# A pool of its own for the second merge's matrices, and two buffers in other PSUM banks for the transposed v, in a hybrid gated-DeltaNet and retention block

## The chip, the cores and the metric

One core of a Trainium2 chip. The metric is the device time of one execution in microseconds (us). Times come from repeated executions and from one profiled execution, whose trace gives every instruction's start, length and cause of waiting. TensorE is PE in what follows (PEld its weight loads), VectorE DVE, ScalarE ACT, GpSimd POOL; SP issues most DMAs.

## The reference, cut to what matters

The layer normalises and projects 1280 tokens (256 of context, 1024 latent), runs a gated delta rule over one group of four heads and a retention over another, projects back, and ends in a SwiGLU. The change sits in the delta rule, between its projections and its scan:

```python
def gated_delta_rule(q, k, v, g, beta):
    ...
    kb = kc * bc[..., None]
    A = jnp.where(strict, jnp.einsum('nbhid,nbhjd->nbhij', kb, kc) * decay, 0.0)
    rhs = jnp.concatenate([vc * bc[..., None], kb * jnp.exp(G)[..., None]], axis=-1)
    sol = lax.linalg.triangular_solve(A + jnp.eye(CHUNK, dtype=A.dtype), rhs,
                                      left_side=True, lower=True, unit_diagonal=True)
    u, w = sol[..., :dv], sol[..., dv:]
    qk = jnp.einsum('nbhid,nbhjd->nbhij', qc, kc) * decay
    ...
    S0 = jnp.zeros((b, h, dk, dv), q.dtype)
    _, o = lax.scan(step, S0, (u, w, q_dec, qk, k_dec, g_last))
```

## The kernel before

The kernel cuts the sequence into ten chunks of 128 tokens and builds, for each chunk, head and direction, a unit triangular 128x128 matrix whose inverse the scan needs. A scheduler in the kernel's language decides the order of the instructions on each engine from the program's text, its pools and its own costs; each engine then runs its list in that order and waits on semaphores. All buffers are tiles of pools; a tag with `bufs=1` has one place, which the next user of the tag gets when every reader of the last one is done.

The stretch that matters lies between the projections of k, q and the retention gate (until about 274 us) and the scan:

- `pre(t)`, once for each chunk. PE multiplies k by itself into PSUM tile `kk` (L665), transposes q into `qt` (L670) and multiplies q by k into `kq` (L675). SP loads a row of decays `gw`; POOL makes the exponent `e` of it (L683, L685), ACT its exponential (L687). DVE multiplies `kk` by `e` into `ut` (L695, four instructions of 128x128 for each direction) and `kq` by `e` into `sp` (L697). `ut` goes to `un` in DRAM, `sp` to the scan's data `sd`. The loads and `gw`, `e`, `sp` live in pool GP.
- `invert(b)`, once for each of three batches of chunks, BATCH = [[0,1,2,9],[3,8,4,7],[5,6]]. Blocks of 32x32 of `un` are reloaded as `yr`, 128 blocks at a time one to a partition, and 31 steps of two DVE instructions (L730, L732) each invert all of them into X. X and its transpose XT go to DRAM `xd` in four stores (L736).
- `merge(b)`, once for each batch. It loads the batch's matrices into tile `U` (L747, up to 2 MB), clears `t64`, and puts the inverted blocks over both with four loads each (L751 into `U`, L752 into `t64`). Then PE joins blocks of 32 to 64 (L771, a DVE copy `xt` L774, L778 and L781) and of 64 to 128 (L794, `xt` L795, L798), ACT copies the results back into `U`, and `U` goes to `sd`. `U` and `t64` have `bufs=1` in pool GM for all three merges.
- Meanwhile the V phase: for each head PE convolves v (L576 to L578, eight weight tiles in three products), DVE adds four taps (L586), ACT applies the silu, PE transposes the result into `vT` (L820), ACT scales it into `vt` (L823) and stores it. `vT` lies in the PSUM banks of `kk`, `qt`, `kq` and the merges (`bank_b`); `vt` has one buffer.
- What can fill PE while it waits: the token-major projections of the output gate and of the retention (L842, L944, L946), matmuls `tm` of 128x256 (L341 to L343), which stand later in the program's text but depend on nothing here but their weights `whi`, `wlo`. 1,276 of them are left at 274 us and are done before the scan is half through. Their three banks are `bank_a`. ACT or DVE reads each out into `res`.

The scan's first loads of `sd` (tile `pk`) follow the merges.

Of the kernel before, what the change touches and what calls it, by code (L numbers as in the profile page):

```python
# [8 lines left out]
F32 = mybir.dt.float32  # L9
# [8 lines left out]
P = 128  # L18
# [7 lines left out]
H = 4  # L26
# [11 lines left out]
def build(nc, tc, ap, dbg=None, stop=None, marks=None):  # L38
# [3 lines left out]
    def pool(name, bufs=1, side=None, space=None):  # L42
        kw = {}
        if side is not None:
            kw["side"] = side
        if space is not None:
            kw["space"] = space
        if space is not DRAM:
            kw["reuse_waits"] = "tile"
        es = ExitStack()  # L50
        p = es.enter_context(tc.tile_pool(name=name, bufs=bufs, **kw))
        root.push(es)
        p_close[id(p)] = es
        return p
# [3 lines left out]
    def close(p):  # L58
        p_close.pop(id(p)).close()
# [5 lines left out]
    def checkpoint(name):  # L65
        if dbg is not None:
            marks.append((name, int(nc.cur_bb.bb.instructions[-1].name.split("-")[-1])))
        if stop == name:
            raise Stop()
# [16 lines left out]
    def bank(tag, name):  # L86
        return PS["pool"].tile([P, 512], F32, tag=tag, name=name, bufs=PS["tags"][tag])

    def bank_a(name):
        return bank("pa", name)  # L90

    def bank_b(name):
        return bank("pb", name)
# [67 lines left out]
    try:  # L161
# [363 lines left out]
        def c8(t, d):  # L525
            return slice(t * 8 + d * 4, t * 8 + d * 4 + 4)
# [17 lines left out]
        ps = bank_b("G")  # L544
# [14 lines left out]
        ps = bank_b("GT")  # L559
# [5 lines left out]
        CV = pool("cv", side="right")  # L565
# [61 lines left out]
        def load(pl, src, tag, bufs, shape=(P, H, P)):  # L627
            x = pl.tile(list(shape), F32, tag=tag, name=tag, bufs=bufs)
            SY.dma_start(x, src)
            return x  # L630
# [17 lines left out]
        checkpoint("rg")  # L648
        close(R2)
        close(W2)  # L650
        GP = pool("gp")
        GU = pool("gu")
        GI = pool("gi")

        BATCH = [[0,1,2,9],[3,8,4,7],[5,6]]
        where = {t: (b, c) for b, ch in enumerate(BATCH) for c, t in enumerate(ch)}
# [3 lines left out]
        def pre(t):  # L660
            b, c = where[t]
            kc = load(GP, kd[t], "kc", 2)
            pk = bank_b("kk")
            for h in range(H):
                T.matmul(pk[:, h * P:(h + 1) * P], kc[:, h, :], kc[:, h, :], start=True, stop=True)  # L665
            if t >= 2:
                qc = load(GP, qd[t - 2], "qc", 2)
                pn = bank_b("qt")
                for h in range(H):
                    T.transpose(pn[:, h * P:(h + 1) * P], qc[:, h, :], ident)  # L670
                for h in range(H):
                    S.activation(pn[:, h * P:(h + 1) * P], pn[:, h * P:(h + 1) * P], AF.Square, accum_out=nq[:, t - 2, h:h + 1])
                pq = bank_b("kq")
                for h in range(H):
                    T.matmul(pq[:, h * P:(h + 1) * P], kc[:, h, :], qc[:, h, :], start=True, stop=True)  # L675
            for d in range(2):
                gw = GP.tile([P, H, P], F32, tag="gw", name="gw", bufs=2)
                SY.dma_start(gw.rearrange("p h i -> p (h i)"),
                             grow_d[c8(t, d), :].rearrange("a b -> (a b)").partition_broadcast(P))
                e = GP.tile([P, H, P], F32, tag="e", name="e", bufs=2)  # L680
                for h in range(H):
                    col = t * 8 + d * 4 + h
                    G.tensor_scalar(e[:, h, :], gw[:, h, :], sm["nG"][:, col:col + 1], 1.0, ALU.add, ALU.mult)  # L683
                sg = 1 if d == 0 else -1
                G.affine_select(out=e, in_=e, compare_op=ALU.is_ge, fill=NEG, base=0,  # L685
                                pattern=[[0, H], [sg, P]], channel_multiplier=-sg)
                S.activation(e, e, AF.Exp)  # L687
                if t >= 2:
                    sp = GP.tile([P, 2, H, P], F32, tag="sp", name="sp", bufs=2)
                ut = GU.tile([P, H, P], F32, tag="ut", name="ut", bufs=2)  # L690
                for h in range(H):
                    col = t * 8 + d * 4 + h
                    hs = slice(h * P, (h + 1) * P)
                    abc_ = sm["ab"][:, col:col + 1]
                    V.scalar_tensor_tensor(ut[:, h, :], pk[:, hs], abc_, e[:, h, :], ALU.mult, ALU.mult)  # L695
                    if t >= 2:
                        V.scalar_tensor_tensor(sp[:, 0, h, :], pq[:, hs], abc_, e[:, h, :], ALU.mult, ALU.mult)  # L697
                SY.dma_start(un[b][:, 1 - d, c * H:(c + 1) * H, :], ut)
                if t >= 2:
                    S.activation(gw, gw, AF.Exp)  # L700
                    G.tensor_tensor(sp[:, 1], gw, qc, ALU.mult)
                    SY.dma_start(sd[t, :, 8 - 8 * d:10 - 8 * d], sp.rearrange("p a h i -> p a (h i)"))
# [5 lines left out]
        def invert(b):  # L708
# [4 lines left out]
            xd = xds[b] = dr.tile([4 * nb, 1024], F32, tag="xd%d" % b, name="xd%d" % b)  # L713
            yr = GI.tile([P, 1024], F32, tag="yr", name="yr", bufs=1)
            for k in range(4):
                SY.dma_start(yr[k:2 * nb:4].rearrange("r (i j) -> r i j", j=32),
                             un[b][q32[k]].rearrange("i e u j -> (e u) i j")[:, :, q32[k]])
            L = GI.tile([P, 1024], F32, tag="L", name="L", bufs=3)
            X = GI.tile([P, 1024], F32, tag="X", name="X", bufs=2)
            G.memset(X, 0.0)  # L720
# [4 lines left out]
            for j in range(31):  # L725
                n = 31 - j
                tmp = GI.tile([P, 256], F32, tag="tmp%d" % b, name="tmp", bufs=2)
                t3 = tmp[:2 * nb, :n * (j + 1)].rearrange("p (i c) -> p i c", c=j + 1)
# [3 lines left out]
                V.tensor_tensor(xs, xs, t3, ALU.subtract)  # L732
            XT = GI.tile([P, 1024], F32, tag="L", name="XT", bufs=3)
            V.tensor_copy(m(XT), X[:2 * nb].rearrange("p (i j) -> p j i", j=32))
# [3 lines left out]
        def blocks(b):  # L738

            nu = len(BATCH[b]) * H  # L740
            nb = 4 * nu

            def blk(dram, k):
                return dram.rearrange("(u b) (i j) -> b i u j", b=4, j=32)[k]

            uu = GM.tile([P, 2, len(BATCH[b]), H, P], F32, tag="U", name="U%d" % b, bufs=1)
            SY.dma_start(uu.rearrange("p e c h j -> p e (c h) j"), un[b])  # L747
            tt = GM.tile([P, 2, nu, 64], F32, tag="t64", name="t64", bufs=1)
            G.memset(tt, 0.0)
            for k in range(4):  # L750
                SY.dma_start(uu[q32[k]].rearrange("p e c h j -> p (e c h) j")[:, :, q32[k]], blk(xds[b][:2 * nb], k))  # L751
                SY.dma_start(tt[q32[k]].rearrange("p e u j -> p (e u) j")[:, :, (k % 2) * 32:(k % 2) * 32 + 32],  # L752
                             blk(xds[b][2 * nb:], k))
            return uu, [uu[:, 1 - d] for d in range(2)], [tt[:, d] for d in range(2)]

        def merge(b):
# [11 lines left out]
            for n in range(nu):  # L768
                for d, p, a, bb in pairs:
                    ca = (a % 2) * 32  # L770
                    T.matmul(ps1[q[bb], n * 32:n * 32 + 32], u[d][q[a], n, q[bb]], t[d][q[a], n, ca:ca + 32],  # L771
                             start=True, stop=True)
            xt1 = GM.tile([P, 16, 32], F32, tag="xt1", name="xt1", bufs=1)
            V.tensor_scalar(xt1.rearrange("p n j -> p (n j)")[:, :nu * 32], ps1[:, :nu * 32], -1.0, None, ALU.mult)  # L774
# [14 lines left out]
            for n0 in range(0, nu, 8):  # L789
                ps1, ps2 = bank_b("m2"), bank_b("m2")  # L790
                xt2 = GM.tile([P, 8, 64], F32, tag="xt2", name="xt2", bufs=1)
                for n in range(8):
# [21 lines left out]
        for h in range(H):  # L814
            y = newy()
            conv_block(8 + h, y, False)
            for t0, n in ((0, 2), (2, 4), (6, 4)):
                ps = bank_b("vT")
                for t in range(t0, t0 + n):
                    T.transpose(ps[:, (t - t0) * P:(t - t0 + 1) * P], y[:, t * P:(t + 1) * P], ident)  # L820
                vt = CV.tile([P, 4, P], F32, tag="vt", name="vt", bufs=1)
                for t in range(n):
                    S.activation(vt[:, t], ps[:, t * P:(t + 1) * P], AF.Copy, scale=sv3[:, t0 + t, h:h + 1])  # L823
                S.dma_start(vd[t0:t0 + n, :, h, :].rearrange("t p j -> p t j"), vt[:, :n])
# [1 line left out]
        checkpoint("v")  # L826
        RP = pool("rp", side="right")
        rope = RP.tile([P, TT, P], F32, tag="rope", name="rope")
        GM = pool("gm")
        for t in BATCH[2]:  # L830
            pre(t)
        checkpoint("pre2")
        merge(0)
        SY.dma_start(rope, ap["rope"])
# [7 lines left out]
            token_major(g, LAT, fin_gate, S, W)  # L842
        checkpoint("rgz")
        close(GM)
        close(GI)
        close(GU)
        close(GP)


        SC = pool("sc", bufs=2, side="right")  # L850
# [764 lines left out]
```

## Time and profile before

| | us |
|---|---|
| three executions | 1484.93, 1485.49, 1488.77 (median 1485.49) |
| the profiled execution | 1486.29 |
| its span, first to last instruction | 1484.5 |
| PE busy | 1406.9 (95% of the span) |
| DVE busy | 974.2 (66%) |
| POOL busy | 628.4 (42%) |
| ACT busy | 604.9 (41%) |
| mean granted TensorE clock | 0.977 of full |

The profiled execution's 1486.29 us is 1.8 us more than its span, and 0.80 us above the median of the three. A span is read by its engines' shares first, and then stretch by stretch: an engine at 95% over the whole has its idle time in a few places, and those are the places where a new order can matter.

### The profile page before, as it was taken

The page shows a single profiled execution, that of the slowest core. Times are in us where ns is not written, and L with a number is a line of the kernel's source. Part 1 is how long each engine was busy: PE and PEld are TensorE (multiplying, and loading weights), DVE is VectorE, ACT ScalarE, POOL GpSimd, SP SyncE. Part 2 cuts the span into 40 slices and gives each one's busy share as a digit, 9 for nine tenths or more (in the row PEclk, how much of TensorE's full clock was granted, in tenths as well). Part 3 has the DMA queues.
Part 4 walks back from the last instruction along what each step waited for, and adds up shares of the span by engine and source line. Part 5 has one row for each costly group of instructions (what it writes and reads, how often), then busy time and mean ns, then how long its engine had stood idle before and what let it go on. Part 6 is the DMA issues. An engine that isn't in the chain of part 4 may idle for free.

```text
span 1484.5 us, 24226 instructions
## 1 busy us (share of the span) xinstructions
PE 1406.9 (95%) x8919; PEld 1206.4 (81%) x8919; DVE 974.2 (66%) x1938; ACT 604.9 (41%) x1268; POOL 628.4 (42%) x581
## 2 busy tenths in 40 slices
PE   7999999987988899999799899999999999999997
PEld 2798888976878899999688688777888888788886
DVE  6566788269868345689767876656555555657486
ACT  5543564375541121245534533323333333444454
POOL 0120011377124343234134689899555553335321
PEclk9999999998999899999899999999999999999999
DMA  8536686578597755996633265765222242776863
GB/s 321 208 99 212 188 250 202 165 233 273 175 266 204 248 186 205 414 361 221 204 114 114 85 207 215 258 243 183 106 107 107 106 144 79 237 278 190 308 204 114
DMA packets 176567, 298.16 MB, mean 201 GB/s; under 512 B 43496, under 2 KB 93880, under 8 KB 172096
## 3 DMA queue, kind: packets, MB, share of 16 engines
q1 hardware_dynamic: 124896, 253.17, 49.5%
q10 hardware_dynamic: 49072, 35.83, 7.7%
q0 software_dynamic: 2480, 7.60, 1.4%
q8 instruction: 70, 1.15, 0.3%
q14 instruction: 49, 0.40, 0.1%
HBM read 206.60 MB, written 89.96 MB: 200 GB/s over the span
## 4 chain that ended last, share of the span: by engine, by line
PE 42%; POOL 4%; DMA 2%; DVE 1%; issue 1%; ACT 0%; SPq 0%; POOLq 0%; ACTq 0%; DVEq 0%
PE ffn L1306 7%; PE ffn L1305 7%; PE ffn L1304 7%; PE fo L1432 4%; PE fo L1430 4%; PE fo L1431 4%; PE op L1163 2%; PE op L1164 2%; PE op L1165 2%; DMA wd<-tw 1%; POOL ws L1277 1%; POOL tw L1358 1%; POOL tw L1357 1%; DVE wlo L315 1%; POOL tw L1359 0%
## 5 line engine op out<-in xcount | busy, mean ns | idle before, releaser
L341 PE MATMUL tm<-whi,hhi 128*128 128x256 f32 (+1 forms) x704 | 201.1, 289 | 5.6 <-ACT xa L354 1.6
L342 PE MATMUL tm<-wlo,hhi 128*128 128x256 f32 (+1 forms) x704 | 201.3, 288 | 0.6 <-DVE wlo L315 0.6
L343 PE MATMUL tm<-whi,hlo 128*128 128x256 f32 (+1 forms) x704 | 199.2, 287 | 0.0
L341 PEld LDWEIGHTS tm<-whi,hhi 128*128 128x128 f32 x704 | 134.0, 191 | 10.0 <-ACT xa L354 2.4
L1304 PE MATMUL ffn<-t,whi 128*128 128x512 f32 x352 | 137.0, 390 | 2.0 <-ACT whi L314 2.0
L1306 PE MATMUL ffn<-t,wlo 128*128 128x512 f32 x352 | 137.1, 390 | 1.5 <-DVE wlo L315 1.5
L1305 PE MATMUL ffn<-t,whi 128*128 128x512 f32 x352 | 137.0, 389 | 0.0
L314 ACT ACTIVATE whi<-wraw 128x512 fp32r<-128x512 f32 (+2 forms) x98 | 75.2, 771 | 151.4 <-PE ffn L1305 80.5
L342 PEld LDWEIGHTS tm<-wlo,hhi 128*128 128x128 f32 x704 | 134.6, 191 | 1.8 <-DVE wlo L315 1.1
L343 PEld LDWEIGHTS tm<-whi,hlo 128*128 128x128 f32 x704 | 134.1, 192 | 1.8 <-issue 0.9
L314 ACT ACTIVATE whi<-ws 128x512 fp32r<-128x512 f32 x88 | 55.6, 632 | 175.4 <-PE ffn L1305 121.6
L315 DVE TENSOR_TENSOR wlo<-ws,whi 128x512 fp32r<-128x512 f32 x88 | 94.3, 1073 | 47.7 <-ACT whi L314 47.5
L1430 PE MATMUL fo<-whi,ahi 128*128 128x512 f32 x308 | 119.3, 390 | 1.3 <-ACT ahi L314 1.3
L1431 PE MATMUL fo<-wlo,ahi 128*128 128x512 f32 x308 | 119.9, 389 | 0.0
L1432 PE MATMUL fo<-whi,alo 128*128 128x512 f32 x308 | 119.0, 390 | 0.0
L315 DVE TENSOR_TENSOR wlo<-wraw,whi 128x512 fp32r<-128x512 f32 (+2 forms) x92 | 100.3, 1092 | 25.0 <-ACT whi L314 25.0
L1304 PE MATMUL ffn<-b,whi 128*128 128x512 f32 x264 | 103.9, 393 | 4.1 <-ACT whi L314 4.1
L1306 PE MATMUL ffn<-b,wlo 128*128 128x512 f32 x264 | 103.9, 394 | 1.1 <-DVE wlo L315 1.1
L1305 PE MATMUL ffn<-b,whi 128*128 128x512 f32 x264 | 103.8, 393 | 0.0
L576 PE MATMUL b<-hhi,whi 128*128 128x512 f32 (+1 forms) x256 | 96.3, 376 | 1.5 <-ACT y L580 1.5
L578 PE MATMUL b<-hhi,wlo 128*128 128x512 f32 (+1 forms) x256 | 95.2, 372 | 0.0
L577 PE MATMUL b<-hlo,whi 128*128 128x512 f32 (+1 forms) x256 | 94.9, 371 | 0.0
(427 smaller groups left out, 3494.6 us busy)
## 6 DMA issues: line engine op xcount, KB each, us to landing
adaw<-ada_w SPq DMA_DIRECT2D x48, 512.0 KB, 4.6
pk<-sd SPq DMA_DIRECT2D x16, 1536.0 KB, 10.1
wraw<-wfi SPq DMA_DIRECT2D x44, 512.0 KB, 4.0
ar<-ad SPq DMA_DIRECT2D x33, 512.0 KB, 4.7
w<-wfo SPq DMA_DIRECT2D x22, 512.0 KB, 4.6
wd<-tw SPq DMA_DIRECT2D x11, 1024.0 KB, 4.8
ad<-act SPq DMA_DIRECT2D x20, 512.0 KB, 3.0
raw<-wd SPq DMA_DIRECT2D x20, 512.0 KB, 4.9
```

The source lines that it names most:

```text
L314: S.activation(hi, raw, AF.Copy)
L315: e.tensor_tensor(lo, raw, hi.bitcast(F32), ALU.subtract)
L341: T.matmul(o, hhi[:, k, tsl], whi[:, k % 4, :], start=(k == 0), stop=False)
L342: T.matmul(o, hhi[:, k, tsl], wlo[:, k % 4, :], start=False, stop=False)
L343: T.matmul(o, hlo[:, k, tsl], whi[:, k % 4, :], start=False, stop=(k == KT - 1))
L576: T.matmul(o, whi[:, k, :], hh, start=(k == 0), stop=False)
L1304: T.matmul(o, whi[:, k, :], xhi(xn, slice(0, 4), k), start=(first and k == 0), stop=False, **kw)
L1305: T.matmul(o, whi[:, k, :], xlo(xn, slice(0, 4), k), start=False, stop=False, **kw)
L1306: T.matmul(o, wlo[:, k, :], xhi(xn, slice(0, 4), k), start=False, stop=(k == 3), **kw)
L1430: T.matmul(po[g][i], ahi[:, ts], whi, start=(j == 0 and not kw), stop=False, **kw)
L1431: T.matmul(po[g][i], ahi[:, ts], wlo, start=False, stop=False, **kw)
L1432: T.matmul(po[g][i], alo[:, ts], whi, start=False, stop=(j == FH - 1), **kw)
```

## The change

It does four things, all in the stretch described. The pools on the left side are opened in the order GU, GI, GP, so that GP is the last; after the last `pre` GP is closed and a new pool G2 opened in its place. The second merge takes its `U` and `t64` from G2 and no longer shares the one place in GM. GM moves to the right side. The transposes `vT` go to `bank_a`, the three banks of the projections, and `vt` has two buffers.

```diff
-        GP = pool("gp")
         GU = pool("gu")
         GI = pool("gi")
+        GP = pool("gp")
...
-            uu = GM.tile([P, 2, len(BATCH[b]), H, P], F32, tag="U", name="U%d" % b, bufs=1)
+            at = G2 if b == 1 else GM
+            uu = at.tile([P, 2, len(BATCH[b]), H, P], F32, tag="U", name="U%d" % b, bufs=1)
             SY.dma_start(uu.rearrange("p e c h j -> p e (c h) j"), un[b])
-            tt = GM.tile([P, 2, nu, 64], F32, tag="t64", name="t64", bufs=1)
+            tt = at.tile([P, 2, nu, 64], F32, tag="t64", name="t64", bufs=1)
...
-                ps = bank_b("vT")
+                ps = bank_a("vT")
...
-                vt = CV.tile([P, 4, P], F32, tag="vt", name="vt", bufs=1)
+                vt = CV.tile([P, 4, P], F32, tag="vt", name="vt", bufs=2)
...
-        GM = pool("gm")
+        GM = pool("gm", side="right")
         for t in BATCH[2]:
             pre(t)
+        close(GP)
+        G2 = pool("g2")
...
         close(GM)
+        close(G2)
         close(GI)
         close(GU)
-        close(GP)
```

Every engine has the same instructions as before; only their order changes. It is the same up to the end of the retention gate's projections and again from the output projection of the delta rule on. Line numbers below the first new line are higher by one, and below the new pool by three.

On PE, at the end of the V phase (`b` is the convolution's bank, `vT` the transposed v), before:

```order
L577 MATMUL b_4048<-hlo,whi 128x512
L578 MATMUL b_4048<-hhi,wlo 128x512
L820 MATMUL vT<-ident,y 128x128 x4
L341 MATMUL tm<-whi,hhi 128x256 x3
L342 MATMUL tm<-wlo,hhi 128x256
L343 MATMUL tm<-whi,hlo 128x256
```

and now:

```order
L821 MATMUL vT<-ident,y 128x128 x10
L665 MATMUL kk<-kc 128x128 x4
L670 MATMUL qt<-ident,qc 128x128 x4
L675 MATMUL kq<-qc,kc 128x128 x4
L665 MATMUL kk<-kc 128x128 x4
L670 MATMUL qt<-ident,qc 128x128 x4
L675 MATMUL kq<-qc,kc 128x128 x4
L821 MATMUL vT<-ident,y 128x128 x10
L341 MATMUL tm<-whi,hhi 128x256
L342 MATMUL tm<-wlo,hhi 128x256
L343 MATMUL tm<-whi,hlo 128x256
```

Before, the first projections `tm` stand among the convolutions, 22 of the 40 transposes and the last two chunks' `kk`, `qt`, `kq` come later among `tm`. Now all of the V phase and all ten chunks stand ahead of the first `tm`; behind these rows 232 `tm` follow in a block, and then merge 0.

On PE, at the first matmuls of the second merge (`m` with its number is that merge's PSUM tile, `t_` and `U_` its matrices), before:

```order
L341 MATMUL tm<-whi,hhi 128x256
L342 MATMUL tm<-wlo,hhi 128x256
L343 MATMUL tm<-whi,hlo 128x256
L771 MATMUL m_4654<-t_4644,U_4642 32x32 x64
L341 MATMUL tm<-whi,hhi 128x256
L342 MATMUL tm<-wlo,hhi 128x256
L343 MATMUL tm<-whi,hlo 128x256
```

and now:

```order
L342 MATMUL tm<-wlo,hhi 128x256
L343 MATMUL tm<-whi,hlo 128x256
L341 MATMUL tm<-whi,hhi 128x256
L799 MATMUL m_4493<-U_4271,xt_4494 64x64 x16
L772 MATMUL m_4658<-t_4648,U_4646 32x32 x64
L342 MATMUL tm<-wlo,hhi 128x256
L343 MATMUL tm<-whi,hlo 128x256
L341 MATMUL tm<-whi,hhi 128x256
```

Before, 128 `tm` stand between merge 0's last L798 and these rows; now there is none, and merge 2 follows merge 1 in the same way.

On SP, from the last `ut` stores to the loads for the first two merges, before (un_2860 to un_2862 are the three batches' matrices, xd_3091 and xd_3494 the inverted blocks of batches 0 and 1):

```order
L698 DMA un_2862<-ut 128x512 x2
L747 DMA U_4267<-un_2860 128x4096
L834 DMA rope<-rope 128x1280
L702 DMA sd<-sp 128x1024
L752 DMA t_4269<-xd_3091 32x32x32 x2
L702 DMA sd<-sp 128x1024
L678 DMA gw<-grow_d 128x512
L752 DMA t_4269<-xd_3091 32x32x32 x2
L751 DMA U_4267<-xd_3091 32x32x32 x2
L698 DMA un_2862<-ut 128x512
L751 DMA U_4267<-xd_3091 32x32x32 x2
L702 DMA sd<-sp 128x1024
```

and now:

```order
L698 DMA un_2862<-ut 128x512
L702 DMA sd<-sp 128x1024
L736 DMA xd_3091<-X 64x1024 x2
L736 DMA xd_3091<-XT 64x1024 x2
L716 DMA yr<-un_2862 16x32x32 x4
L752 DMA U_4271<-xd_3091 32x32x32 x2
L753 DMA t_4273<-xd_3091 32x32x32 x2
L752 DMA U_4271<-xd_3091 32x32x32
L753 DMA t_4273<-xd_3091 32x32x32
L752 DMA U_4271<-xd_3091 32x32x32
L753 DMA t_4273<-xd_3091 32x32x32
L748 DMA U_4646<-un_2861 128x4096
```

Before, the loads for merge 0 stand between stores of `sp` and a load of `gw` that belong to the last two chunks. Now all of those stores are ahead of inversion 0's stores, and merge 0's eight loads follow them directly. The second merge's load of its 2 MB (U_4646) now stands ahead of inversion 1's stores, where before it stood behind them and behind four loads into `t`.

## Rows read from the trace of the kernel before

**Rows 1.** Busy time by stretch: PE, PEld, DVE, ACT, POOL, granted clock, DMA share, GB/s.

```profile
340.00:360.00 20.00, 11.96 (x84) 10.82 (x82) 18.26 (x50) 12.69 (x30) 15.41 (x26) 0.86 0.83 287
...
420.00:440.00 20.00, 13.69 (x377) 12.48 (x375) 17.44 (x48) 7.77 (x11) 4.78 (x7) 0.83 1.04 279
...
480.00:500.00 20.00, 14.14 (x287) 13.26 (x286) 7.92 (x24) 3.42 (x6) 4.71 (x11) 0.74 0.71 236
```

**Rows 2.** PE's waits over the span: for what, total us, times, longest us.

```profile
PE m L778 <- DMA U<-xd: 4.0, 2, 3.0
PE m L771 <- DMA t<-xd: 3.9, 3, 2.6
...
PE m L781 <- issue: 2.7, 2, 1.8
...
PE m L771 <- DMA U<-un: 2.2, 1, 2.2
...
PE tm L341 <- ACT res L502: 1.5, 1, 1.5
...
PE m L798 <- DVE xt L795: 1.1, 1, 1.1
```

**Rows 3.** Groups of DVE's instructions, 283 to 374 us: busy, mean ns, idle before.

```profile
L586 DVE SCALAR_TENSOR_TENSOR y<-u,cw,y 128x1022 f32<-128x1022 f32 (+3 forms) x25 | 25.3, 1036 | 2.3 <-ACT y L580 2.3
L695 DVE SCALAR_TENSOR_TENSOR ut<-kk,ab,e 128x128 f32<-128x128 f32 x64 | 19.1, 341 | 32.1 <-ACT e L687 32.1
L697 DVE SCALAR_TENSOR_TENSOR sp<-kq,ab,e 128x128 f32<-128x128 f32 x48 | 14.6, 340 | 0.0
L730 DVE TENSOR_TENSOR tmp<-L,X 128x240 f32<-128x240 f32 (+15 forms) x20 | 8.7, 435 | 2.1 <-ACT L L723 1.7
L732 DVE TENSOR_TENSOR X<-X,tmp 128x247 f32<-128x247 f32 (+15 forms) x19 | 7.3, 384 | 0.4
```

**Rows 4.** ACT and POOL in order of time around the first `e`.

```profile
271.27 1.22 POOL L685 TENSOR_SCALAR_AFFINE_SELECT e<-e 128x512 f32<-128x512 f32 x2
...
282.50 1.15 ACT L687 ACTIVATE e<-e 128x512 f32<-128x512 f32 x2
```

**Rows 5.** SP's queue in order of time: stores of batches 0 and 1, merge 1's loads.

```profile
386.13 1.15 SPq L736 DMA_DIRECT2D xd<-X  x2
387.38 2.14 SPq L736 DMA_DIRECT2D xd<-XT  x2
...
438.76 1.09 SPq L736 DMA_DIRECT2D xd<-X  x2
...
456.62 3.99 SPq L752 DMA_DIRECT2D t<-xd  x4
...
474.24 4.17 SPq L751 DMA_DIRECT2D U<-xd  x4
```

**Rows 6.** Line L736, stores of X and XT, issue to landing.

```profile
DMA to landing us min/median/max: 2.1/3.5/5.3
```

**Rows 7.** Line L752, loads of `t64`, issue to landing.

```profile
DMA to landing us min/median/max: 3.4/5.2/5.4
```

**Rows 8.** PE in order of time: two `tm` in a run, and two pieces of merges.

```profile
425.05 0.28 PE L342 MATMUL tm<-wlo,hhi 128*128 128x256 f32 x1
425.17 0.28 PE L343 MATMUL tm<-whi,hlo 128*128 128x256 f32 x1
...
455.80 1.15 PE L798 MATMUL m<-U,xt 64*64 64x64 f32 x32
...
474.47 1.28 PE L771 MATMUL m<-t,U 32*32 32x32 f32 x128 [2.22 <-DMA U<-un]
```

**Rows 9.** PE in order of time: a transposed v, and a chunk's `kk` twice.

```profile
395.25 0.66 PE L820 MATMUL vT<-ident,y 128*128 128x128 f32 x4 [1.60 <-ACT vt L823]
...
399.62 1.05 PE L665 MATMUL kk<-kc 128*128 128x128 f32 x8
```

## The prediction

> **What bounds the kernel now.** The table of times comes first: PE is busy 1406.9 of 1484.5 us, so the change can only win or lose what PE stands still, or runs slowly, in the stretch whose order changes. The table of stretches shows where that is. Between 340 and 360 us PE is busy 11.96 of 20 while DVE is busy 18.26; between 420 and 440 it is busy 13.69 at a granted clock of 0.83, and between 480 and 500 14.14 at 0.74 [rows 1]. The first is in the V phase, where DVE has to multiply each `kk` and `kq` before their banks are free again. What the others are, the list of PE's waits says: L771 and L778, the first steps of a merge, wait for `t<-xd`, `U<-xd` and `U<-un`, for handoffs by DRAM [rows 2]. SP's queue tells why these are late. Inversion 1's X is stored at 438.8 us, but merge 1's four loads into `t64` are issued from 456.62 on and its four into `U` from 474.24 [rows 5], since the one place of each was merge 0's until then.
>
> **The V phase.** In the new order all ten chunks and all of the V phase lie ahead of the first `tm`, so PE gets there when DVE has let it. Call that time T; before, the long run of `tm` begins at about 373.7 us, and I measure from there.
>
> From its first `ut` at 283 us until 374 DVE did 25 of 28 taps, 64 + 48 of 128 `ut` and `sp`, and 39 half-steps of inversion 0 (20 and 19 of them in 8.7 and 7.3 us, 0.41 us each) [rows 3]. In the new order DVE does 28 taps, 112 `ut` and `sp` and only 25 half-steps, the earlier and shorter ones, before the last tap of V. So it has 3 us more of taps, at 25.3/25 each; the 14 half-steps less are 6 us, at 0.41. That is 3 us less in all, and I count 1 of them, since now the last chunks stand closer together and share POOL.
>
> And DVE starts earlier. Before, POOL had finished the first two `e` at 272.5 us, and ACT took them at 282.50, behind results `res` that came before it in its list [rows 4]. In the new order ACT takes them ahead of the last four `res`, so DVE begins at about 276.5 instead of 283.2. The price, two more loads of ACT's tables between `res`, makes PE wait 2 us there at most, but ahead of a phase in which it waits for DVE anyway, so I count nothing; without that cover it costs those 2 us. So the last tap ends at 373.7 - 6.7 - 1 = 366; the last silu and ten transposes take some 5 more: T = 371. The bounds are 364 (all 3 us, and transposes hidden) and 380 (no earlier start that helps, because POOL or ACT sets the pace).
>
> At T the new order is ahead by 22 transposes and 24 matmuls of two chunks, at 0.13 us each (eight in 1.05, [rows 9]) 6.0 us, and behind by the 36 `tm` that before had done, at 0.118 us (pitch of neighbours, [rows 8]) 4.2 us. With 2.7 us for T itself that is 4.5 us ahead. But PE comes out of a waiting stretch with no `tm` as filler: between 340 and 360 the clock was 0.86 beside 8 us of idling [rows 1], and I charge 2 us more at half clock than before. **V phase: -2.5 us**, bounds -9 and +8. The two buffers of `vt` and its new banks take away waits that lie either behind T, counted next (1.60 us, [rows 9]), or ahead of it, where DVE ends last.
>
> **What goes away behind T.** PE's idle time from 374 to 488 us is the sum of 4.0, 3.9, 2.7, 2.2, 1.5 and 1.1 [rows 2] and of the 1.6 for `vt`: 17.0 us. The granted clock costs 0.17 of 13.69 busy and 0.26 of 14.14, 2.3 and 3.7 us [rows 1]. All of it belongs to the old places of `vT` and of merges 0 and 1: **-23.0 us**.
>
> **What comes in its place.** Now 232 `tm` stand between T and merge 0, and none between one merge's last matmuls and the next one's first. A merge's own work on PE is about 7.8 us: 1.28 for L771, the same by count for the 96 of L778 and L781 (1.9), and four blocks at 1.15 [rows 8]; some 115 `tm` inside it are 13.5 us.
>
> A handoff runs so: X is done on DVE; four stores are issued in 3.4 us [rows 5] and land 3.5 us after [rows 6]; eight loads are issued at 1 us each [rows 5]; the last lands 5.2 us after issue [rows 7]. A first load can go when the first store has landed, so I take 19 us for a big batch. For batch 2, half as large, I take 14.
>
> Merge 0: behind the last tap DVE has 18 steps of inversion 0 (36 half-steps at 0.41, 14.8 us) and 16 `ut` and `sp` (19.1/64 each, 4.8), 20 us from the last tap, so X is done at T + 15 and its last load has landed at T + 34 to 35. PE is at the merge's first pair at T + 27.4 (232 at 0.118), and at its last block 56 `tm` later. I take 3 us of waiting (0 to 5).
>
> Merge 1: inversion 1 starts 2 us after X, runs 26 us (62 half-steps at 0.41 or a little more), and DVE does two weight differences and one `xt` between: X at T + 46, data at T + 65. PE is there at T + 27.4 + 6.6 + 3 + 13.5 + 7.8 + 1 = T + 59, and now needs everything at once, 64 matmuls in a row. 6 us (0 to 9).
>
> Merge 2: X at T + 80, data at T + 94; PE at the block that needs all of it at T + 90. 4 us (0 to 8).
>
> Waits for `xt`, with DVE inverting at the same time: 2 us (before 1.1, [rows 2]). Waits of such length brought a clock of 0.83 in a stretch of 20 us [rows 1], 2.4 us at a busy share of 0.7; two of them cost 4.8. The scan's first `pk` now loads behind merge 2's handoff instead of ahead of it: 1 us (0 to 5, the longest landing in [rows 6] once). **Together +20.8 us.**
>
> The Trainium skill, "DMA: Bandwidth & Descriptors", section "Anatomy of one DMA — SWDGE (gpsimd) path", gives a fixed cost of about 2.0 us and bytes at 436 GB/s on top, about 2.3 us (an estimate by that page) for a load of 128 KB. It is written for the other issuing path, and here such loads landed after 5.2 us, so the measurement decides; by the rule a handoff would be some 4 us shorter, and the sum about 10 us lower.
>
> **The sum**: -2.5 - 23.0 + 20.8 = -4.7 us on the profiled execution's 1486.29, so 1481.6. That execution is 0.80 above the median of the three, 1485.49; on the median it is **1480.8 us**.
>
> **The rivals.**
>
> *The matrices come in time.* With handoffs at the shortest rows, 2.1 us for a store and 3.4 for a load [rows 6, 7], each is 3.2 us shorter: merge 0 waits nothing, merge 1 3, merge 2 1, `xt` 2, one slow stretch 2.4, 1 for `pk`: +9.4 and a sum of -16.1, 1469. With every new wait gone it is 1460. For it: SP's queue is free of other stores at that place, and the load of 2 MB is out of the way early. Against it: at 420 to 440 us the DMA share was 1.04 [rows 1], and stores of results go on.
>
> *The V phase ends late.* PE has no `tm` to fill it, and every wait for `ut` is now paid in full. At T = 380 everything behind moves by 9 us and the slow stretch grows by 2: +6, 1492. For it: DVE at 18.26 of 20 [rows 1] leaves little to catch up with. Against it: DVE had that share with `tm` as filler too. It decides from T = 379 on, where the sum passes +4.5.
>
> *It does not do what it says.* The second merge's wait was put down to the one place of `U`, but inversion 1 itself ends late, and the wait only changes its name. If the three new waits are 9, 6 and 4 instead of 6, 4 and 3, the sum is +1 and nothing is to be seen: 1487.
>
> **How the numbers follow.** The forecast has 0.42 (its own range 1475 to 1486), the first rival 0.27, the second 0.22, the third 0.09. The three executions lie 3.8 us apart, and 0.3%, 4.5 us, is about what a measurement can tell from no change. The forecast lies at that bound: 0.23 of it is faster, 0.18 the same, 0.01 slower. The first rival gives 0.26 faster and 0.01 the same; the second 0.17 slower and 0.05 the same; the third 0.07 and 0.02. That makes 0.49 faster, 0.31 the same, 0.20 slower. The range goes from 1466, where most of the first rival's handoffs are in time, to 1494, a T a little past 380 with the waits kept; about one in ten is left out on either side.
>
> **What would show it.** In the changed kernel's trace: the first `ut` near 276 us; the first run of `tm` at about 371 and none between the gate's projections and it; inversion 0's X stored near 386, inversion 1's near 417; waits of L772 or L779 for `U<-xd` or `t<-xd` of about 3, 6 and 4 us, at about 401, 433 and 463; `U<-un` of merge 1 in no list of waits; from the scan on a constant shift of about -5 us. The prediction is wrong if T is off by more than 5 us, or if PE meets the merges' matrices without waiting.

## The result, and the profile after

The changed kernel takes 1493.10 us (median of 15 executions, 1484.53 to 1501.62) against 1485.49 for the kernel before (15 executions, 1482.27 to 1489.06): a ratio of 1.0044, with a 95% interval of 1.0024 to 1.0064. It is 3.6 to 9.5 us slower; I had forecast 4.7 us faster. The same kernel in a second comparison, on the chip of experiments 5 to 8, gave 1.0034 (1.0015 to 1.0053). (The ratios here and below are formed over the executions; they are not the quotients of the two medians.)

Its executions lie 17 us apart, those of before 7. So one profile does not stand for the kernel: the first profiled execution took 1501.62 us, the slowest of all, a second one (experiment 8) 1489.25. Both are read below, and the second lies nearer to the medians of the two comparisons, 1493.10 and 1491.59.

The table of stretches, cut at the last `vT`, the end of merge 2 and the start of the output projection. The columns are the stretch, its length, then busy us (and instructions) of PE, PEld, DVE, ACT and POOL, the granted clock, DMA share and GB/s. Before (cut at the long run of `tm` at 374):

```profile
256.00:374.00 118.00, 103.62 (x616) 90.76 (x615) 76.41 (x186) 62.68 (x138) 69.14 (x104) 0.91 0.66 213
374.00:537.00 163.00, 145.36 (x2102) 140.14 (x2101) 103.60 (x273) 50.23 (x107) 51.70 (x86) 0.95 0.72 216
537.00:718.00 181.00, 171.04 (x1457) 168.25 (x1456) 130.62 (x471) 62.95 (x175) 60.41 (x78) 0.98 0.78 289
```

After, first profile:

```profile
256.00:378.00 122.00, 102.63 (x630) 89.53 (x629) 85.89 (x199) 74.99 (x178) 74.30 (x109) 0.93 0.74 234
378.00:510.00 132.00, 108.58 (x1758) 103.42 (x1758) 81.53 (x214) 35.26 (x65) 26.11 (x41) 0.91 0.74 214
510.00:734.00 224.00, 210.40 (x1775) 206.53 (x1775) 142.70 (x516) 64.53 (x176) 84.19 (x122) 0.98 0.68 251
```

After, second profile:

```profile
256.00:378.00 122.00, 102.74 (x627) 89.74 (x626) 85.84 (x199) 74.87 (x177) 75.21 (x109) 0.92 0.73 231
378.00:498.00 120.00, 107.11 (x1764) 102.11 (x1763) 79.69 (x214) 35.30 (x65) 26.09 (x41) 0.94 0.83 239
498.00:722.00 224.00, 210.74 (x1778) 206.72 (x1777) 142.33 (x516) 64.33 (x176) 84.30 (x122) 0.98 0.68 250
```

Length less PE's busy time is what PE stood still. Before: 14.4, 17.6 and 10.0 us, 42 in all. After: 19.4, 23.4 and 13.6, 56 in all; in the second profile 19.3, 12.9 and 13.3, 45 in all. The first and the last stretch are worse in both (the merges end earlier now, so the last is 43 us longer than before and holds more of the projections). The middle one, where the merges lie, varies: it holds 10.5 of the 12 us between the two profiles, and in the second it is shorter than before's 17.6.

PE's waits in the first profile (for what: total us, times, longest):

```profile
PE kk L665 <- ACT qt L672: 9.4, 4, 5.6
PE m L772 <- DMA t<-xd: 9.1, 3, 4.2
...
PE m L779 <- issue: 4.8, 1, 4.8
PE vT L821 <- ACT y L589: 4.3, 2, 2.2
...
PE tm L342 <- DVE wlo L315: 3.9, 2, 3.5
PE tm L341 <- ACT res L502: 3.4, 2, 1.9
```

Against [rows 2] the wait for `U<-un` is gone, and so is that for `U<-xd` by name; in their place PE waits for `t<-xd`, the inverted blocks themselves, and in the V phase for ACT. The place of the second merge's matrices is free early, as the change intends: their load `U<-un` is issued at 416.2 us, before at 464.6. What comes late is the inverted blocks, whose X is ready at 433.8 (before 438.8).

### The profile page after: what moved, and what is told of

The parts are those of the page before. It is cut to its first block, busy times and chain, and to the rows that moved or that the text cites. A ratio compares the mean times of both kernels' runs of the same rounds, so it can differ in the third digit from the quotient of the medians.

```text
span 1499.8 us, 24212 instructions
## 1 busy us (share of the span) xinstructions
PE 1407.4 (94%) x8919; PEld 1207.5 (81%) x8919; DVE 973.0 (65%) x1938; ACT 605.6 (40%) x1268; POOL 629.9 (42%) x581
## 4 chain that ended last, share of the span: by engine, by line
PE 69%; DVE 10%; DMA 10%; issue 4%; POOL 4%; ACT 3%; SPq 1%; ACTq 0%; DVEq 0%; POOLq 0%
PE ffn L1309 8%; PE ffn L1308 8%; PE ffn L1307 8%; PE fo L1434 4%; PE fo L1433 4%; PE fo L1435 4%; PE tm L342 4%; PE tm L341 4%; PE tm L343 4%; PE b L576 2%; PE b L578 2%; PE b L577 2%; PE op L1168 2%; PE op L1166 2%; PE op L1167 2%
```

## The experiments

Times are medians; ratios are against the kernel before on the same chip, with 95% intervals. "Still" is PE's idle time in the three stretches, cut at the same events.

**The two halves.** The change has a half on the transposed v (its banks, a second buffer) and a half on the pools. Each alone:

```diff
-                ps = bank_b("vT")
+                ps = bank_a("vT")
...
-                vt = CV.tile([P, 4, P], F32, tag="vt", name="vt", bufs=1)
+                vt = CV.tile([P, 4, P], F32, tag="vt", name="vt", bufs=2)
```

> The change's half on the transposed v alone: its banks and its second buffer; the pools stay as before. In this kernel's order no projection stands among the convolutions (the first run of them, 34 and then 229, begins behind the last transposes), and 141 and 130 projections stand between the merges, as before. Theory 1 (the loss is in the V phase and right behind it: without projections as filler PE pays DVE's and ACT's pace, and leaves the phase at half clock): 4 to 10 us slower than before, first run of projections at 375 to 380 us, waits for merges' matrices no longer than before's 10.1 us in all. Theory 2 (the loss is at the merges, which follow one another without projections between): within 3 us of before, since the merges stand apart here.

Measured: 1480.66 us, 0.9973 (0.9961 to 0.9985). Faster by 4 us, so theory 1 has the wrong sign; theory 2's range of 3 us about before is passed by one.

The other half is the rest of the diff shown ahead of the prediction.

> The change's half on the pools alone: the second merge's matrices in a pool of their own, the transposed v in its old banks with one buffer. In this order 36 projections stand in the V phase as before, and merge 1 follows merge 0 with none between. Theory 1: 0 to 8 us faster than before, the V phase as before (run of projections at about 374 us). Theory 2: 4 to 10 us slower than before, with 6 us or more of waiting at merge 1's first matmuls and PE's clock at half there.

Measured: 1504.14 us, 1.0133 (1.0117 to 1.0149). Slower by 19 us, twice what theory 2 had at most, and L772's waits for `t<-xd` are 5.5 us in all, where it had 6 or more at merge 1 alone. The two halves do not add up (+15 by the medians, +7.6 together), but their signs are clear. Theory 1 falls by the first run: in the half on the transposed v, PE stands still 22.3 us in the V phase, 8 more than before, and 8.3 at the merges, 9 less. Its three stretches:

```profile
256.00:381.00 125.00, 102.73 (x615) 91.44 (x613) 76.29 (x180) 71.81 (x167) 74.73 (x110) 0.90 0.71 221
381.00:529.00 148.00, 139.68 (x2044) 134.44 (x2042) 101.12 (x269) 39.88 (x77) 42.69 (x72) 0.95 0.71 219
529.00:715.00 186.00, 175.27 (x1510) 172.40 (x1506) 133.38 (x479) 62.90 (x175) 65.22 (x86) 0.99 0.77 283
```

The projections that were not spent in the V phase stand in front of and between the merges, and cover their handoffs. The three sums of standing still are 41.3 us against 42.0 before, though, and the stretches are 3 us shorter: the rest is shorter busy time, whose cause the rows do not name. In the half on the pools the merges are not covered (from 375 us to merge 2's end):

```profile
375.00:520.00 145.00, 122.23 (x1816) 116.08 (x1816) 91.50 (x234) 49.66 (x107) 30.38 (x50) 0.85 0.76 224
```

22.8 us of standing still, and a clock of 0.85 where before had 0.95. The V phase is no better than before either, with 18.2 us against 14.4.

**Variants of the half on v.** The pools' half with the second buffer, which is the changed kernel with `vT` back in its old banks:

```diff
-                ps = bank_a("vT")
+                ps = bank_b("vT")
```

> The pools' half and the second buffer of the scaled v, but the transposed v in its old banks: of the whole change only the banks are undone. 36 projections stand in the V phase, and ahead of merge 0 all 64 of its first matmuls stand in one block. Theory 1: 2 to 10 us faster than the changed kernel, and no slower than before. Theory 2: like the changed kernel, 4 to 10 us slower than before.

Measured: 1502.90 us, 1.0123 (1.0109 to 1.0138). That is 18 us slower than before, more than either theory had. Against the half on the pools it is 1 us, within the spread of four executions each.

The changed kernel with `vT` in the convolution's banks:

```diff
-                ps = bank_a("vT")
+                ps = bank_c("vT")
```

> The changed kernel with the transposed v in the convolution's two banks in place of the projections' three, so that projections may stand ahead of the last transposes again: in this order 36 do, and then 88, but the chunks' first products stand in larger groups. Theory 1: faster than the changed kernel by 3 to 10 us, if the convolution's banks don't become a wait of their own. Theory 2: like the changed kernel within 3 us, since merges follow one another here too.

Measured: 1514.00 us, 1.0197 (1.0182 to 1.0211), the slowest of all. Now the chunks crowd together early, and PE waits 15.7 us for `ut` before a `qt` and stands still 33.9 us in all until 385. That a filler may stand there does not help when something else is put in the wrong place. Both theories miss: the first had a gain, the second the changed kernel's time within 3 us.

With the pools as before, the new banks without a second buffer:

```diff
-                ps = bank_b("vT")
+                ps = bank_a("vT")
```

> Of the half on the transposed v the banks alone: the projections' three banks, still one buffer for the scaled v; pools as before. No projection stands in the V phase, 137 and 126 stand between the merges. If the gain of the half (1480.66 us against 1485.04) comes from the banks: 1478 to 1484 us. If it needs the second buffer: 1485 us or more, with PE waiting for the scaled v in the V phase by more than 3 us.

Measured: 1485.84 us, 1.0005 (0.9993 to 1.0017). The banks alone give nothing: PE stands still 22.8, 9.6 and 14.2 us, the gain at the merges being paid for on both sides. The forecast that it needs the second buffer holds in time, but not by the wait that it named: PE's wait in the V phase is 13.2 us before a `vT` for ACT's `y`, and none for `vt` is listed.

The same with three buffers:

```diff
-                vt = CV.tile([P, 4, P], F32, tag="vt", name="vt", bufs=1)
+                vt = CV.tile([P, 4, P], F32, tag="vt", name="vt", bufs=3)
```

> The half on the transposed v with three buffers for the scaled v instead of two; pools as before. 154 and 134 projections stand between the merges. If the scaled v's store still holds up ACT, and by it the V phase: 1474 to 1480 us, faster than the half with two buffers (1480.66). If DVE alone sets the pace there: 1479 to 1483 us.

Measured: 1480.01 us, 0.9963 (0.9949 to 0.9977), the best version found, with the pools as before. Against two buffers it is not told apart.

**What of the pools' half costs.** Two parts: the place of its own, and the new order of the pools (with GM's side). One word undoes the first:

```diff
-            at = G2 if b == 1 else GM
+            at = GM
```

in the changed kernel, and in the pools' half alone:

> The changed kernel with one thing undone: the second merge's matrices take the shared place in GM again; the pools' order, GM's side and the transposed v stay as changed, the new pool stays empty. The order is that of the changed kernel up to the middle of merge 0, and then 149 and 114 projections stand between the merges. Theory 2 (a place of its own lets the merges be put one right behind the other, ahead of their data, and takes the projections from between them): 1476 to 1486 us, as the half on the transposed v alone (1480.66), at least 7 us faster than the changed kernel; merges' matrices waited for less than 6 us in all. Theory 3 (the loss comes from the pools' new order and its queues, not from the merges): 1490 us or more.

Measured: 1486.38 us, 1.0006 (0.9989 to 1.0024), against 1491.59 for the changed kernel on the same chip. Giving the place back is worth 5 us, less than the 7 expected.

> Only the pools' order and GM's side are changed; second merge's matrices in the shared place, transposed v in its old banks with one buffer. 139 and 121 projections stand between the merges. Theory 2: 1481 to 1490 us, as before within 0.4%, some 15 us faster than the half on the pools. Theory 3: 1498 us or more, as the half on the pools (1504).

Measured: 1495.19 us, 1.0070 (1.0049 to 1.0091). That falls between both theories' numbers: the order of the pools costs by itself, some 9 us, and the place of its own another 9. With the new half on the transposed v both cost less. Each run against its own runs of before, the way from before to the changed kernel is -0.27% (that half, experiment 1), +0.33% (the order of the pools, experiment 5) and +0.28 to 0.38% (the place of its own): about -4, +5 and +5 us, each uncertain by 2 or 3. The order of the pools again, for a second profile:

> Only the pools' order and GM's side again, for a second profile beside the others: 1492 to 1498 us; more waiting than before of PE for the transposed and scaled v (some 10 us between 350 and 375) and for results at the start of merge 0 (5 us), if these are the pools' order and not chance.

Measured: 1494.04 us, 1.0066 (1.0044 to 1.0089). PE's waits, second profile:

```profile
PE vT L821 <- ACT vt L824: 9.7, 4, 5.1
PE tm L341 <- ACT res L502: 8.2, 2, 5.5
PE m L782 <- issue: 5.5, 3, 2.5
PE kk L665 <- ACT qt L672: 5.2, 1, 5.2
```

These are the same waits in both profiles (10.7, 6.9, 5.5 and 5.7 in the first), so they are the order's and not chance. PE stands still 20.5 and 20.4 us until 375, against 14.4 before, and 21.1 and 21.6 from there to merge 2's end, against 17.6. Whether the first row is the cause is not shown: the second buffer of experiment 3, which should remove it, left 6.3 us of it, where the half on the pools has 8.7.

**What the place of its own does.** It lets the scheduler put the merges right behind one another; whether they then stand there for lack of data, this tells (of the two changed lines the part that changes):

```diff
-blk(xds[b][:2 * nb], k)
+blk(xds[0][:2 * nb], k)
...
-blk(xds[b][2 * nb:], k)
+blk(xds[0][2 * nb:4 * nb], k)
```

> The changed kernel, but merges 1 and 2 read the inverted blocks of batch 0, which are there long before, in place of their own: the wait for inversions 1 and 2 is taken away (the two inversions are still done and stored), and the merges still follow one another, with none or some 26 projections between. Theory 2: 8 to 16 us faster than the changed kernel, 1477 to 1485 us, with under 2 us of waiting for loads at merges 1 and 2. If the loss is in something else of the merges standing close (ACT, DVE, banks): within 4 us of the changed kernel's 1493.

Measured: 1477.92 us, 0.9943 (0.9924 to 0.9963), 14 us faster than the changed kernel on the same chip. No wait for `t<-xd` or `U<-xd` is left. With the data there, the kernel is faster than before although the merges follow one another; so the changed kernel's loss at the merges is the inversions' data, which they meet too early. What merges that stand apart would gain by such data is not shown.

> The changed kernel once more, unedited, for a second profile and beside the others on one chip: 1488 to 1497 us. Theory 2: the waits of merges' first matmuls for loads and the stretches at half clock are at the merges again, 8 us of waiting or more between merge 0 and merge 2.

Measured: 1491.59 us, 1.0034 (1.0015 to 1.0053). In this profile:

```profile
PE m L772 <- DMA t<-xd: 4.8, 3, 2.1
...
PE m L772 <- issue: 3.0, 2, 2.0
...
PE m L779 <- issue: 2.4, 2, 2.2
```

The wait is there, but not 8 us by name (the rows with "issue" have no releaser in the profile), and the mean clock from T to merge 2's end is 0.94 instead of 0.91.

**Why the data are late.** Does DVE end the V phase?

```diff
-                    if t >= 2:
-                        V.scalar_tensor_tensor(sp[:, 0, h, :], pq[:, hs], abc_, e[:, h, :], ALU.mult, ALU.mult)
+                if t >= 2:
+                    V.tensor_tensor(sp[:, 0], pq.rearrange("p (h i) -> p h i", i=P), e, ALU.mult)
```

> The changed kernel with less work for DVE in the V phase: the four instructions that scale the product of q and k for each chunk and direction are one without the factor beta, some 0.45 us less each time, 16 times, 7 us in all; the output lacks that factor. The order is that of the changed kernel (231 projections ahead of merge 0). If DVE sets the V phase's end: the first run of projections begins at 370 to 373 us instead of 377.5, and the time falls by 4 to 8 us to 1484 to 1489. If ACT's queue or POOL sets it: less than 2 us earlier, and the time within 3 us of 1493.

Measured: 1486.80 us, 1.0005 (0.9995 to 1.0016), some 5 us less than the changed kernel on other chips, but the V phase did not end earlier. DVE has 79.7 us of work until 378 instead of 85.8, the last `vT` ends at 379.2 (377.6 and 378.7 in the changed kernel), and the wait that ends last is for ACT:

```profile
PE kk L665 <- ACT qt L672: 8.9, 3, 7.8
PE vT L821 <- ACT y L589: 7.5, 4, 2.3
```

So the time fell as if DVE set the phase's end, but less work for DVE did not end the phase earlier. What was saved early was lost at 315 us, in a wait for `e`, and from 340 to 378 DVE is busy 36.4 of 38 us, as in the changed kernel (36.2 and 37.0). The gain came behind the phase, at the inversions. DVE:

```profile
315.00 1.13 DVE L695 SCALAR_TENSOR_TENSOR ut<-kk,ab,e 128x128 f32<-128x128 f32 x4 [6.03 <-ACT e L687]
```

Inversion 0's X is copied at 392.7 us, in the changed kernel at 399.4 and 395.3, and inversion 1's at 430.6 (433.8 and 432.8); L772's wait for `t<-xd` is 1.2 us instead of 9.1 and 4.8.

And does a copy hold up inversion 1? In the changed kernel DVE's list has merge 0's `xt` in the midst of inversion 1's steps, and DVE stands there until PE has done L772, which PE comes to behind its 232 projections. DVE, first profile, and below it the same copy in the second:

```profile
426.94 0.69 DVE L775 TENSOR_SCALAR xt<-m 128x512 f32<-128x512 f32 x1 [5.28 <-PE m L772]
...
433.84 1.13 DVE L734 COPY XT<-X 128x1024 f32<-128x1024 f32 x1
```

```profile
425.87 0.69 DVE L775 TENSOR_SCALAR xt<-m 128x512 f32<-128x512 f32 x1 [7.49 <-PE m L772]
```

The experiment gives both copies to ACT (one of the two is shown):

```diff
-                V.tensor_scalar(xt2.rearrange("p n j -> p (n j)"), ps1, -1.0, None, ALU.mult)
+                S.activation(xt2.rearrange("p n j -> p (n j)"), ps1, AF.Copy, scale=-1.0)
```

> The changed kernel with the merges' copies xt made by ACT in place of DVE, the same values. Up to merge 0's first matmuls the order is that of the changed kernel; DVE's list now holds inversion 1 without a copy in its midst. If the copy's wait for merge 0 holds inversion 1 up: X of inversion 1 is stored 5 to 8 us earlier than in the changed kernel (433.8 and 432.8 us), at about 427, PE waits 3 to 6 us less for loads at merge 1, and the time is 1482 to 1489. If DVE's own pace does it: stored within 2 us of 433, and the time within 3 us of 1492.

Measured: 1483.76 us, 0.9985 (0.9971 to 0.9999), 8 us faster than the changed kernel's 1491.59, though on another chip; both against their own runs of before 0.5%. Inversion 1's X is done ten us earlier, and merge 1's first step waits for nothing. From inversion 0's X to inversion 1's it takes 29.7 us, against 34.4 and 37.5 in the changed kernel's profiles, so 5 to 8 us of the ten are the copy's; the others are there at inversion 0 already. DVE, and then PE:

```profile
423.35 1.09 DVE L734 COPY XT<-X 128x1024 f32<-128x1024 f32 x1
```

```profile
444.03 1.29 PE L772 MATMUL m<-t,U 32*32 32x32 f32 x128
```

(No bracket: no idle time before it.) In the best version the same edit costs time:

> The half on the transposed v with three buffers (1480.0 us), and the copies xt made by ACT. The merges stand 132 and 126 projections apart here, so inversion 1 has time: within 3 us of 1480, 1477 to 1483, if the wait behind xt costs only where the merges follow one another; 1476 or less if it costs here too.

Measured: 1487.33 us, 1.0014 (1.0000 to 1.0028), 7 us more than the best version had, and outside both ranges expected. Inversion 1's X is earlier here too, at 426.1 us instead of 435.0, but the merges' waits do not get shorter (10.7 us in all, against 8.9): L778 4.9 us without a releaser, `U<-xd` 2.5, `U<-un` 2.4. So where merges stand apart DVE's wait is not the bound; why the edit costs 7 us, ACT's new work or something else, is not shown.

## Why the prediction was wrong

**Where the kernel was bound.** Right: everything happened between 256 and 734 us, and the kernel behind it kept a constant shift.

**The V phase, -2.5 us.** This step failed. T was to be 371; the first run of `tm` began at 377.49, in the second profile at 378.36, and a T off by more than 5 us was one of the prediction's own signs of being wrong. By its working that is +4 to +5 instead of -2.5. The failing line is "So the last tap ends at 373.7 - 6.7 - 1 = 366" (it ended at 374.7): I moved a whole loop by its start. DVE in the first profile:

```profile
277.66 2.16 DVE L695 SCALAR_TENSOR_TENSOR ut<-kk,ab,e 128x128 f32<-128x128 f32 x8 [19.23 <-PE kk L665]
283.68 2.16 DVE L695 SCALAR_TENSOR_TENSOR ut<-kk,ab,e 128x128 f32<-128x128 f32 x8 [3.86 <-DMA un<-ut]
287.92 1.13 DVE L695 SCALAR_TENSOR_TENSOR ut<-kk,ab,e 128x128 f32<-128x128 f32 x4 [2.08 <-ACT e L687]
...
305.58 1.13 DVE L695 SCALAR_TENSOR_TENSOR ut<-kk,ab,e 128x128 f32<-128x128 f32 x4 [2.79 <-ACT e L687]
...
313.49 3.34 DVE L586 SCALAR_TENSOR_TENSOR y<-u,cw,y 128x1022 f32<-128x1022 f32 x1 [4.31 <-ACT y L580]
```

It starts early, at 277.7, nearly as forecast, and then stands 3.9 us for its own store to land (`ut` has two buffers), 2.1 and 2.8 for `e`, 4.3 for what ACT makes of a convolution; the second profile has the same waits. By 314 the lead is gone: DVE has then made 32 `ut` and 17 taps, in the kernel before 31 and 17. Experiment 11 shows the other side: with 6 us less work for DVE the phase ends no earlier. The phase is a loop through PE, DVE, ACT, POOL and stores, and DVE's start and amount of work alone do not give its end.

**What goes away behind T, -23.0 us.** The old waits did go, as far as they were the old places': `U<-un` before merge 1 is in no list.

**What comes in its place, +20.8 us.** The merges' waits were right in kind and near in size: forecast 3, 6 and 4 us and 2 for `xt`, 15 in all; the waits of L772 and L779 are 15.0 us in the first profile and some 10 in the second. Merge 1, which PE reached at T + 70 where T + 59 was forecast, has most of them in the first profile:

```profile
450.44 0.24 PE L772 MATMUL m<-t,U 32*32 32x32 f32 x2 [2.69 <-DMA t<-xd]
454.85 1.91 PE L772 MATMUL m<-t,U 32*32 32x32 f32 x122 [4.17 <-DMA t<-xd]
468.03 0.21 PE L779 MATMUL m<-U,xt 32*32 32x32 f32 x1 [4.84 <-issue]
```

What failed is the way there. The 232 `tm` ahead of merge 0 were counted at 0.118 us each, 27.4 us, as if PE were free to run them at full clock. From T to merge 0's first matmul it took 39.2 us in the first profile and 34.0 in the second (columns as in the table of stretches):

```profile
377.49:416.68 39.19, 32.57 (x234) 31.83 (x232) 31.22 (x82) 13.07 (x25) 12.26 (x16) 0.87 0.87 241
```

```profile
378.36:412.32 33.96, 31.23 (x234) 30.62 (x232) 27.86 (x78) 12.77 (x25) 12.07 (x16) 0.90 0.89 260
```

So 12 and 7 us were lost where the sum has nothing. 4 to 5 of them are busy time above 27.4 us, beside a granted clock of 0.87 and 0.90, and the others waits, in the first profile 1.6 us for ACT's `vt`, 1.6 for `res` and 3.5 for the weights `wlo`, which stand behind inversion 0 in DVE's list:

```profile
409.26 0.58 PE L342 MATMUL tm<-wlo,hhi 128*128 128x256 f32 x1 [3.48 <-DVE wlo L315]
```

Two smaller terms failed too. Inversion 1's X was done at T + 56 (T + 54 in the second profile) and not at T + 46. Part of that is inversion 0, whose X came at T + 22 and T + 17 instead of T + 15, in the first profile behind 5.9 us of waiting for `e`:

```profile
387.02 0.35 DVE L695 SCALAR_TENSOR_TENSOR ut<-kk,ab,e 128x128 f32<-128x128 f32 x1 [5.92 <-ACT e L687]
```

The other part is `xt`, which makes DVE wait 5.3 and 7.5 us for PE in the midst of inversion 1: I had counted it as work, without naming what is queued behind it. And the stretch behind the merges stood still 3.6 and 3.3 us more than before (13.6 and 13.3 against 10.0), where I had 1.

Put into the prediction's sum, an estimate from these figures for the first profile: T +6.5, the 232 `tm` +11.8, the last stretch +2.6 on -4.7 make +16; it was +15.3 against the profile of before. In the second profile the same way gives +7, with 5 us less of waits at the merges, and +3.0 was measured.

**The rivals.** That the time came out as the second rival's (1492, T at 380) is chance: T stays under the 379 from which that rival decides, experiment 11 has T at 379.1 and is faster than the changed kernel, and experiment 1, with the old pools, has T at 381 and is faster than before. The third rival, that the place was not what the second merge waited for, is nearer to what happened; its price was put too low, since it did not reckon that merges in a row hold up the next inversion. Experiments 5 and 7 show it from both sides. The first rival is excluded by the same rows. The rule of the Trainium skill that was weighed ("DMA: Bandwidth & Descriptors", section "Anatomy of one DMA — SWDGE (gpsimd) path"), about 2.3 us (an estimate by that page) for a load of 128 KB, would have made the merges' waits shorter still. The trace does not agree: in the changed kernel the loads into `t64` landed 4.5 us after issue in the median and 8.2 at most, in the second profile 5.1 and 8.0.

**Stays open.** Why the new order of the pools costs some 9 us by itself (experiments 6 and 12), and some 5 beside the new half on the transposed v. Every engine does the same work in a different order in the V phase; the waits are repeatable, but no single one was taken away. So of the changed kernel's loss only the part of the second place is traced to its cause. And the profile names no releaser for several waits inside the merges (4.84 us at L779 above).

## What to carry to other kernels

A buffer of its own removes a wait only if the buffer is what comes last; look for the time at which its content is made before giving memory for it. Where a scheduler orders the work, such a place also lets it move the waiting work ahead of the filler, and the same wait is then paid on the engine that is the bound: see how many filler instructions stand between producer and consumer before and after. And when a consumer's step sits in the producer's queue (here a 0.7 us copy among an inversion's steps), the consumer's wait becomes the next producer's delay. Moving that step away is not a gain everywhere: the same edit gained 8 us in one order and cost 7 in another.

## What the runs showed of the hardware

That the granted clock falls beside PE's waits in this stretch. In the first profile it was at half of full speed, 1.2 of 2.4 GHz, in three pieces between the start of the 232 projections and the last merge. They begin at 408.4, 452.7 and 466.4 us, each during one of the waits of 3.5, 4.2 and 4.8 us shown above. The columns are those of the table of stretches:

```profile
409.00:415.00 6.00, 5.74 (x27) 5.74 (x28) 5.66 (x14) 0.39 (x1) 0.00 (x0) 0.50 1.12 194
453.00:459.00 6.00, 4.15 (x133) 4.08 (x134) 1.88 (x5) 0.00 (x0) 0.00 (x0) 0.50 0.65 228
467.00:473.00 6.00, 4.97 (x44) 4.90 (x44) 4.67 (x17) 3.42 (x6) 0.00 (x0) 0.50 0.02 5
```

The mean of that stretch was 0.91, against 0.94 in the second profile, where the waits were shorter. So two profiles of one program differ by 10.5 us of PE's standing still in the stretch of the merges and by the clock on top.

The changed kernel's 15 executions lie 17 us apart, those of before 7. That it is the merges in a row which widen the spread is not shown: experiment 5, with projections between them again, lies 14.7 us apart in 12 executions, and experiments 2, 3 and 4, with merges in a row, 3 us in four each.
